# Modulation of the opening stage by unsplit fp32 products for five of eight channel tiles, a held engine order there, and transposes for the later modulation sums

## The chip, the cores and the metric

The kernel runs on one core of a Trainium2 chip. The metric is the time of one execution on that core in microseconds (us), as the median of the runs shown. The engines are named as the profile names them: PE (TensorE, the matrix engine) and PEld (its weight loads), DVE (VectorE), ACT (ScalarE), POOL (GpSimd) and SP (the queue that issues most transfers). SBUF is the core's working memory and PSUM the memory into which PE writes.

## What is computed

A two-layer backbone over 256 latent tokens and 256 context tokens of 1024 channels, all in fp32. Each layer has a modulated norm, a projection to a pooling branch and two attention branches, a gated merge, and a gated MLP. What the change touches is the modulation:

```python
mod   = (silu(c)     @ w_mod[l] + b_mod[l]).reshape(Bn, 6, 1, D_MODEL)
mod_c = (silu(c_ctx) @ w_mod[l] + b_mod[l]).reshape(6, 1, 1, D_MODEL)
h  = rms_norm(x, norm1_g[l])   * (1 + mod[:, 1]) + mod[:, 0]
hc = rms_norm(ctx, norm1_g[l]) * (1 + mod_c[1])  + mod_c[0]
z, zc = h @ w_in[l], hc @ w_in[l]
```

`w_mod` is 1024 by 6144 for each layer. There are two conditioning vectors, `c` and `c_ctx`, so every modulation value is a product of a matrix with two vectors.

## The kernel before

Tokens lie along the free axis (512 of them, latent then context, 256 each) and channels along the 128 partitions, in eight tiles of 128 channels. A large product is made in three passes of fp32r operands: weights are split into a high part `wH` (ACT, line 188) and a low part `wL` (line 190, on DVE or POOL), the normalised stream into `hH` (ACT, 470) and `hL` (DVE, 471), and `mm3` (205 to 207) adds high by high, high by low and low by high.

**Opening stage.** It turns `x` and `ctx` into channel tiles (`ptx`, 605; copies `xs`, 606), sums their squares on ACT (608), and forms the reciprocal root of the mean by three Newton steps (`rsqrt`, here on POOL, 294 to 297). `spread_b` (313, tile `rBp`) spreads the roots over the partitions. `rows_turn` (132) turns the biases into columns (`pt_a`). For each channel tile j, `first_mod(j)` loads 2 units of `w_mod` (512 rows by 256 columns: 128 columns of shift, 128 of scale), splits them, and multiplies: the conditioning vectors, 4 columns of high and low parts (`cHL`), are the weights, and 256 columns of `w_mod` stream, 16 products in all (`pm`, 344 and 345). ACT copies the 4 rows out (`mrow`, 348), PE turns them (`mt`, 357), and DVE adds bias and one and multiplies by the norm's gain (`mod`, 361 and 364). `start_apply(j)` makes `hu` (468), `hH` and `hL` of the tile, and the tile's part of the projection of the window branch (`pq` 512 wide, `pkv` 256 wide, 24 products for each tile) follows. The code runs `first_mod` up to two tiles ahead of the projection. `run_program` walks the list of steps, issues loads some units ahead (`MORE`) and splits `AHEAD` = 2 units ahead. The unit's number decides the engine of its low part: in this stage DVE, and POOL for numbers 5, 7 and 8:

```python
eng = pool_e if (self.idx % 4) in ONPOOL[self.lay] or self.idx in FPOOL else dve
```

A scheduler of the framework sets the order of each engine's instructions within the data's dependencies; `after` adds an order between two instructions of one engine.

**Later modulation.** The other 4 groups of layer 0 and all 6 of layer 1 are computed in the background of other products (`Background`): DVE multiplies and adds blocks of `w_mod` into `ma`, 128 partitions by 512 columns (431, 433), and `fin` sums over the partitions with 4 products by a column of ones (447, PSUM tile `mpt`), whose 4 columns DVE then finishes (453 to 460). `fin` runs 32 times. Its PSUM tile comes from a pool of two banks that transposes and spreads share (`psT`).

Of the kernel before, what the change touches and what calls it, by code (L numbers as in the profile page):

```python
# [32 lines left out]
ORD = 6  # L33
FPOOL = (5, 7, 8)
# [8 lines left out]
def kernel(  # L43
# [116 lines left out]
    lastop = {}  # L160
# [5 lines left out]

    class Unit:
        def __init__(self, load, kt, cols, first=False):
            self.load, self.kt, self.cols, self.first, self.loaded = load, kt, cols, first, False
            self.lay = now[0]  # L170
            self.uses, self.idx, self.H, self.L, self.side = 0, None, None, None, False

# [8 lines left out]
        def split(self):  # L181
# [36 lines left out]
    def run_program():  # L218
        units, loads, seen = [], [], set()
        cur = 0  # L220
        for need, _ in prog:
            for u in need:
                u.uses += 1
                if id(u) not in seen:
                    seen.add(id(u))
                    if u.side:
                        loads.append((cur + SIDE, u))
                    else:
                        cur = u.idx = len(units)
                        units.append(u)  # L230
                        loads.append((cur, u))
# [21 lines left out]
        for need, fn in prog:  # L253
# [5 lines left out]
            if started or need:  # L259
                split_to(cur + 1 + AHEAD)  # L260
# [11 lines left out]
    AHEAD = 2  # L272
# [15 lines left out]
    def rsqrt(v, n, name="rs", apart=False):  # L288
        r = small(n, f"{name}_r", 2)
        lastop["magic"] = dve.tensor_scalar(r.bitcast(I32), v.bitcast(I32), -0.5, float(0x5F3759DF), op0=ALU.mult, op1=ALU.add)  # L290
        t = small(n, f"{name}_t", 2)
        for _ in range(3):
            if apart:
                pool_e.tensor_tensor(out=t, in0=r, in1=r, op=ALU.mult)
                pool_e.tensor_tensor(out=t, in0=t, in1=v, op=ALU.mult)
                pool_e.tensor_scalar(t, t, -0.5, 1.5, op0=ALU.mult, op1=ALU.add)
                pool_e.tensor_tensor(out=r, in0=r, in1=t, op=ALU.mult)
            else:
                dve.tensor_tensor(out=t, in0=r, in1=r, op=ALU.mult)
# [1071 lines left out]
```

## Time and profile before

| | |
|---|---|
| median of 3 runs | 1394.54 us (1388.57 to 1395.63) |
| the profiled execution: its own time, its span | 1393.51 us, 1391.6 us |
| PE busy, DVE, ACT, POOL | 95%, 60%, 48%, 41% of the span |
| chain of work that ended last: PE, DVE, ACT | 78%, 11%, 4% |
| first product of the projection, first product after it | 35.10 us, 83.88 us |
| granted clock of PE over the span | 0.982 of full speed |

Busy shares are means over stages. The chain tells which engine's work the end waited for; the timeline of an engine tells when it started what and, in brackets, how long it had been idle and for whom; a table of stretches gives busy time and granted clock (0.50 is 1.2 GHz, 1.00 is 2.4 GHz). Records of PE overlap: the cost of one is the distance of the starts of neighbours, not its length. An fp32 product with fp32 weights shows as two records, one with fp32r operands and a transpose as one.

### The profile page before, as it was taken

How to read it: one execution, taken by the hardware profiler on the slowest of the kernel's cores; microseconds unless marked ns; L12 is line 12 of the kernel's file. 1: busy time of each engine (PE TensorE's matmuls, PEld its weight loads, DVE VectorE, ACT ScalarE, POOL GpSimd, SP SyncE). 2: the span in 40 equal slices, each digit the busy share in tenths (PEclk: the TensorE clock that was granted, in tenths of full speed). 3: DMA queues.
4: the chain of work that ended last, by engine and by line, in shares of the span. 5: the costliest groups of instructions: out<-in, count | busy, mean ns of one | idle time of the engine just before them, and what ended most of it. 6: DMA issues, size and time to landing. Idle time of an engine off the chain costs nothing.

```text
span 1391.6 us, 21515 instructions
## 1 busy us (share of the span) xinstructions
PE 1320.5 (95%) x8133; PEld 1160.0 (83%) x8133; DVE 841.8 (60%) x1766; ACT 664.6 (48%) x1238; POOL 573.8 (41%) x317
## 2 busy tenths in 40 slices
PE   4999899989999999999999999998999998999997
PEld 3877678868888898888888888987898898999997
DVE  6779965587765667766644333478818845544422
ACT  4558652257633344433433222457745854555442
POOL 4421223452234434444444343453246154566553
PEclk8999999999999999999999999999999998999999
DMA  9711124532135544555654554543154156466653
GB/s 282 234 39 61 61 81 139 174 92 93 61 119 150 176 132 121 167 157 163 182 165 151 160 174 152 163 142 120 54 144 140 58 180 184 135 183 183 197 160 99
DMA packets 174087, 195.75 MB, mean 141 GB/s; under 512 B 6878, under 2 KB 147830, under 8 KB 173728
## 3 DMA queue, kind: packets, MB, share of 16 engines
q1 hardware_dynamic: 173088, 193.23, 45.3%
q0 software_dynamic: 896, 1.14, 0.4%
q8 instruction: 64, 1.05, 0.3%
q14 instruction: 39, 0.32, 0.1%
HBM read 191.21 MB, written 3.15 MB: 140 GB/s over the span
## 4 chain that ended last, share of the span: by engine, by line
PE 78%; DVE 11%; ACT 4%; issue 3%; DMA 2%; POOL 2%; SPq 0%; ACTq 0%; POOLq 0%; DVEq 0%
PE gp L205 21%; PE gp L206 20%; PE gp L207 20%; PE mpt L447 2%; PE S L865 2%; PE ptp L906 2%; POOL wL L190 1%; PE pq L205 1%; DMA raw<-in_w_mod_dram 1%; PE pq L206 1%; DVE pr L895 1%; PE pq L207 1%; ACT wH L188 1%; PE O L206 1%; PE O L205 1%
## 5 line engine op out<-in xcount | busy, mean ns | idle before, releaser
L190 POOL TENSOR_TENSOR wL<-raw,wH 128x1024 fp32r<-128x1024 f32 (+2 forms) x233 | 541.9, 2330 | 773.1 <-ACT wH L188 685.5
L188 ACT ACTIVATE wH<-raw 128x1024 fp32r<-128x1024 f32 (+2 forms) x294 | 293.6, 1001 | 364.1 <-PE gp L206 177.7
L205 PE MATMUL gp<-hH,wH 128*128 128x512 f32 (+1 forms) x1168 | 394.8, 340 | 4.1 <-ACT hH L470 1.5
L206 PE MATMUL gp<-hL,wH 128*128 128x512 f32 (+1 forms) x1168 | 392.2, 336 | 1.6 <-DVE hL L471 1.6
L207 PE MATMUL gp<-hH,wL 128*128 128x256 f32 (+1 forms) x1168 | 391.5, 336 | 2.2 <-POOL wL L190 1.4
L205 PEld LDWEIGHTS gp<-hH,wH 128*128 128x128 f32 x1168 | 221.9, 191 | 25.8 <-ACT hH L470 2.3
L207 PEld LDWEIGHTS gp<-hH,wL 128*128 128x128 f32 x1168 | 222.4, 191 | 25.0 <-POOL wL L190 1.8
L206 PEld LDWEIGHTS gp<-hL,wH 128*128 128x128 f32 x1168 | 222.8, 191 | 22.8 <-DVE hL L471 2.7
L433 DVE SCALAR_TENSOR_TENSOR mb<-raw,cs,mb 128x512 f32<-128x512 f32 x182 | 131.0, 751 | 109.8 <-DMA raw<-in_w_mod_dram 108.9
L205 PE MATMUL gp<-g,wH 128*128 128x256 f32 (+1 forms) x396 | 128.1, 324 | 0.0
L206 PE MATMUL gp<-g,wH 128*128 128x256 f32 (+1 forms) x396 | 127.6, 322 | 0.0
L207 PE MATMUL gp<-g,wL 128*128 128x256 f32 (+1 forms) x396 | 127.4, 322 | 0.0
L190 DVE TENSOR_TENSOR wL<-raw,wH 128x1024 fp32r<-128x1024 f32 (+2 forms) x61 | 71.0, 1166 | 83.3 <-ACT wH L188 73.2
L207 PEld LDWEIGHTS gp<-g,wL 128*128 128x128 f32 x396 | 75.8, 191 | 6.1
L206 PEld LDWEIGHTS gp<-g,wH 128*128 128x128 f32 x396 | 75.9, 192 | 5.9
L205 PEld LDWEIGHTS gp<-g,wH 128*128 128x128 f32 x396 | 75.7, 191 | 5.9
L876 ACT ACTIVATE pr<-S,nm 128x512 f32<-128x512 f32 (+1 forms) x96 | 58.6, 611 | 18.2 <-DVE nm L871 9.9
L205 PE MATMUL gp<-y,wH 128*128 128x512 f32 (+1 forms) x192 | 67.3, 351 | 0.0
L207 PE MATMUL gp<-y,wL 128*128 128x512 f32 (+1 forms) x192 | 65.5, 342 | 1.0 <-POOL wL L190 1.0
L206 PE MATMUL gp<-y,wH 128*128 128x512 f32 (+1 forms) x192 | 65.9, 343 | 0.0
L871 DVE TENSOR_REDUCE nm<-S 128x1 f32<-128x512 f32 (+1 forms) x96 | 56.7, 594 | 10.4 <-PE S L865 7.4
L202 DVE TENSOR_TENSOR pL<-ptp,pH 128x512 fp32r<-128x512 f32 (+1 forms) x96 | 57.0, 595 | 7.1 <-ACT pH L201 6.6
(213 smaller groups left out, 2292.2 us busy)
## 6 DMA issues: line engine op xcount, KB each, us to landing
raw<-in_w_mod_dram SPq DMA_DIRECT2D x80, 512.0 KB, 3.8
raw<-in_w_gate_dram SPq DMA_DIRECT2D x48, 512.0 KB, 3.5
raw<-in_w_ff_gate_dram SPq DMA_DIRECT2D x44, 512.0 KB, 4.0
raw<-in_w_ff_val_dram SPq DMA_DIRECT2D x44, 512.0 KB, 3.9
raw<-in_w_ff_down_dram SPq DMA_DIRECT2D x44, 512.0 KB, 3.6
raw<-in_w_in_dram SPq DMA_DIRECT2D x32, 384.0 KB, 3.4
raw<-in_w_branch_dram SPq DMA_DIRECT2D x24, 512.0 KB, 3.4
raw<-in_w_mod_dram SPq DMA_DIRECT2D x32, 256.0 KB, 6.1
```

What stands on the lines that cost most here:

```text
L188: h = act.activation(out=self.H, in_=self.raw, func=AF.Copy)
L190: lo = eng.tensor_tensor(out=self.L, in0=self.raw, in1=self.H.bitcast(F32), op=ALU.subtract)
L202: dve.tensor_tensor(out=Lo, in0=src, in1=H.bitcast(F32), op=ALU.subtract)
L205: recent.append(pe.matmul(o, lhsT=aH, rhs=bH, start=first, stop=False))
L206: pe.matmul(o, lhsT=aH, rhs=bL, start=False, stop=False)
L207: pe.matmul(o, lhsT=aL, rhs=bH, start=False, stop=last)
L433: dve.scalar_tensor_tensor(out=S["a"][s], in0=raw, scalar=cs[:, s, k:k + 1], in1=S["a"][s], op0=ALU.mult, op1=ALU.add)
L447: pe.matmul(red[:, m:m + 1], lhsT=S["a"][s][:, m * P:(m + 1) * P], rhs=ones, start=(m == 0), stop=(m == 3))
L865: pe.matmul(S, lhsT=self.hd.qT[t][:, h], rhs=self.hd.kT[:, kv * 2 + v, koff:koff + nkey], start=(v == 0), stop=(v == 1 and not msk))
L871: dve.tensor_reduce(out=nm, in_=S, axis=AX.X, op=ALU.max, negate=True)
L876: act.activation(out=pr[:, :nkey], in_=S, func=AF.Exp, scale=0.125 if self.window else 1.0, bias=nm, accum_out=ls)
L906: pe.transpose(pt[:, k], pr[:, k * P:(k + 1) * P], ident)
```

## The change

For channel tiles 0, 1, 2, 4 and 6 (`PLAIN`) the weights of the modulation are no longer split. Blocks of 128 by 128 of raw `w_mod` are the weights of 16 fp32 products whose moving operand is the two conditioning vectors (`pmc`, 2 columns); the sums come out in channel order, so copy, turn and their additions fall away and two instructions on DVE finish them (`fin0`). Tiles 3, 5 and 7 keep the split. The order is held on PE (`pin`) and for the splits (`turned`, `hold`): the modulation of tile j + 1 stands inside the projection of tile j, after two of its four token blocks (after one for a split tile, whose turn follows one block later). Loads go by tile: `w_mod` of tile j, then `w_in` of tile j. The Newton steps go to DVE, the biases are turned before them, and the spread roots of tile 0 are read from PSUM. POOL splits nothing in this stage. The store of the stream to memory moves from tile 2 to tile 5 (`SPILL`). Later, `fin` turns its 4 blocks by transposes into a whole bank and DVE sums them (`tensor_reduce`). Since unsplit units are no longer numbered, the numbers of all later units fall by 10, which turns the pattern by which layer 1 gives low parts to POOL or DVE.

```diff
-ORD = 6
-FPOOL = (5, 7, 8)
+
+PLAIN = (0, 1, 2, 4, 6)
...
+    def pin(mm, at):
+        if at and "pe" in lastop:
+            after(mm, lastop["pe"])
+        lastop["pe"] = mm
...
-            eng = pool_e if (self.idx % 4) in ONPOOL[self.lay] or self.idx in FPOOL else dve
+            eng = pool_e if (self.idx % 4) in ONPOOL[self.lay] else dve
             lo = eng.tensor_tensor(out=self.L, in0=self.raw, in1=self.H.bitcast(F32), op=ALU.subtract)
-            if self.idx < ORD:
-                after(h, lastop["sq"])
-                if eng is dve:
-                    after(lo, lastop["magic"])
+            if self.tile is not None:
+                after(h, turned.get(max(turned) if self.first else self.tile - 1, lastop["sq"]))
+                after(lo, lastop["hold"])
...
                     if u.side:
-                        loads.append((cur + SIDE, u))
+                        loads.append((cur + SIDE if u.key is None else u.key, u))
                     else:
-                        cur = u.idx = len(units)
+                        u.idx = len(units)
+                        cur = u.idx if u.key is None else cur
                         units.append(u)
-                        loads.append((cur, u))
+                        loads.append((u.idx if u.key is None else u.key, u))
...
-            if started or need:
-                split_to(cur + 1 + AHEAD)
+            if started or any(not u.side for u in need):
+                split_to(cur + 1 + ahead[0])
...
-            if apart:
-                pool_e.tensor_tensor(out=t, in0=r, in1=r, op=ALU.mult)
...
+            dve.tensor_tensor(out=t, in0=r, in1=r, op=ALU.mult)
+            dve.scalar_tensor_tensor(out=t, in0=t, scalar=-0.5, in1=v, op0=ALU.mult, op1=ALU.mult)
+            lastop["hold"] = dve.scalar_tensor_tensor(out=r, in0=t, scalar=1.5, in1=r, op0=ALU.add, op1=ALU.mult)
...
+            w = Unit(load, 4, 256, True)
+            w.side, w.key, w.tile = plain, j - 0.5, j
+            return w
+
+
+        def step0(u, w):
+            def fn():
+                if u == 0:
+                    S["pm"] = psT((P, 2, 2), name="pmc")
+                for k in range(4):
+                    kk = u * 4 + k
+                    for i in range(2):
+                        mm = pe.matmul(S["pm"][:, i], lhsT=w.raw[:, k, i * P:(i + 1) * P], rhs=csv[:, kk],
+                                       start=(kk == 0 and i == 0), stop=(kk == KT - 1 and i == 1))
+                        pin(mm, k == 0 and i == 0)
+                lastop["mods"] = mm
+            return fn
...
+        def fin0():
+            dve.tensor_scalar(modv[0][0][:, j], S["pm"][:, 0], colsA[0][:, j:j + 1], None, op0=ALU.add)
+            dve.tensor_scalar(modv[0][1][:, j], S["pm"][:, 1], late["b1"][:, j:j + 1],
+                              colsA[0][:, 48 + j:49 + j], op0=ALU.add, op1=ALU.mult)
...
-                red = psT((P, 4), name="mpt")
+                pt = psT((P, 4, P), name="mpt")
                 for m in range(4):
-                    pe.matmul(red[:, m:m + 1], lhsT=S["a"][s][:, m * P:(m + 1) * P], rhs=ones,
-                              start=(m == 0), stop=(m == 3))
+                    pe.transpose(pt[:, m], S["a"][s][:, m * P:(m + 1) * P], ident)
+                red = small(4, "mred", 2)
+                dve.tensor_reduce(out=red, in_=pt, axis=AX.X, op=ALU.add)
...
-        r = spread_a(ssum, 4, True)
+        colsA[0] = rows_turn(*arow0)
+        late["b1"] = cst.tile([P, KT], F32, name="b1")
+        dve.tensor_scalar(late["b1"], colsA[0][:, KT:2 * KT], 1.0, None, op0=ALU.add)
+        late["r"] = spread_a(ssum, 4)
+
+    def start_spread():
+        pb = spread_b(late["r"], 4)
         for s in range(2):
-            pb = spread_b(r[:, 2 * s:2 * s + 2], 2)
             rB = sp0.tile([P, 256], F32, name=f"rB{s}")
-            act.activation(out=rB, in_=pb, func=AF.Copy)
+            act.activation(out=rB, in_=pb[:, s * 256:(s + 1) * 256], func=AF.Copy)
             rBs.append(rB)
-        colsA[0] = rows_turn(*arow0)
+        late["pb"] = pb
...
-    SPILL = 2
+    SPILL = 5
...
-                apply_h(j, slice(s * 256, (s + 1) * 256), s, modv[0][1], modv[0][0], rBs[s])
+                apply_h(j, slice(s * 256, (s + 1) * 256), s, modv[0][1], modv[0][0],
+                        rBs[s] if j else late["pb"][:, s * 256:(s + 1) * 256])
...
+    mods, fin = first_mod(0)
+    extend(mods[:1])
+    add(start_spread)
+    extend(mods[1:])
+    add(fin)
     add(start_apply(0))
-    fins[1] = first_mod(1)
     for j in range(KT):
-        if j + 2 < KT:
-            fins[j + 2] = first_mod(j + 2)
+        steps = proj_w.steps(j)
+        at = 2 if j + 1 in PLAIN else 1
+        extend(steps[:at])
+        if j == KT - 1:
+            add(lambda: ahead.__setitem__(0, 2))
         if j + 1 < KT:
-            add(fins[j + 1])
+            mods, fin = first.pop(j + 1, None) or first_mod(j + 1)
+            extend(mods)
+            if j + 1 not in PLAIN:
+                extend(steps[at:at + 1])
+                at += 1
+            elif j + 2 < KT and j + 2 not in PLAIN:
+                first[j + 2] = first_mod(j + 2)
+                for need, _ in first[j + 2][0]:
+                    add(lambda: None, need)
+            add(fin)
             add(start_apply(j + 1))
-        extend(proj_w.steps(j))
+        extend(steps[at:])
```

PE at the beginning, from the last `x` transposes on. `pm` are the split products, `pmc` the unsplit ones, the numbers behind `raw`, `wH` and `wL` those of buffers. Before:

```order
L605 MATMUL ptx<-ident,xn_158 128x128 x8
L313 MATMUL rBp<-ident,rs_r 128x128 x4
L132 MATMUL pt_a_245<-ident,rows_a_121 128x92
L344 MATMUL pm<-wH_267,cHL 4x256
L345 MATMUL pm<-wL_268,cHL 4x256
...
L345 MATMUL pm<-wL_345,cHL 4x256
L205 MATMUL pq<-wH,hH_99 128x512
L357 MATMUL mt<-ident,mrow 128x4 x2
```

Now:

```order
L638 MATMUL ptx<-ident,xn_158 128x128 x8
L132 MATMUL pt_a_218<-ident,rows_a_121 128x92
L351 MATMUL pmc<-cs,raw_238 128x2 x8
L317 MATMUL rBp<-ident,rs_r 128x128 x4
L351 MATMUL pmc<-cs,raw_241 128x2 x8
L211 MATMUL pq<-wH,hH_99 128x512
...
L215 MATMUL pkv<-wH,hL_107 128x256
L351 MATMUL pmc<-cs,raw_246 128x2 x8
L351 MATMUL pmc<-cs,raw_249 128x2 x8
L211 MATMUL pq<-wH,hH_99 128x512
```

Three tiles' modulation stood ahead of the first projection product; now one does, and the next tile's lies between the halves of the projection.

DVE in the same stretch, up to the first `hu`. Before:

```order
L307 TENSOR_SCALAR nv<-xss 128x4
L290 TENSOR_SCALAR rs_r<-nv 128x4
L190 TENSOR_TENSOR wL_268<-raw_249,wH_267 128x1024
...
L190 TENSOR_TENSOR wL<-raw,wH 128x768
L359 COPY mt<-mt 128x8
L361 SCALAR_TENSOR_TENSOR mod_0_139<-mt,cols_a_247 128x2
L361 SCALAR_TENSOR_TENSOR mod_1_140<-mt,cols_a_247 128x2
L364 TENSOR_SCALAR mod_1_140<-mod_1_140,cols_a_247 128x2
L468 SCALAR_TENSOR_TENSOR hu<-xs,mod_1_140,rB_238 128x256
```

Now:

```order
L134 COPY cols_a_220<-pt_a_218 128x92
L311 TENSOR_SCALAR nv<-xss 128x4
L645 TENSOR_SCALAR b_222<-cols_a_220 128x8
L300 TENSOR_SCALAR rs_r<-nv 128x4
L719 TENSOR_SCALAR bgh_862<-cols_a_220 128x24
L303 TENSOR_TENSOR rs_t<-rs_r 128x4
...
L305 SCALAR_TENSOR_TENSOR rs_r<-rs_t,rs_r 128x4
L378 TENSOR_SCALAR mod_0_139<-pmc,cols_a_220 128x2
L379 TENSOR_SCALAR mod_1_140<-pmc,b_222,cols_a_220 128x2
L499 SCALAR_TENSOR_TENSOR hu<-xs,mod_1_140,rBp 128x256 x2
```

The low parts have left the stretch ahead of `hu`, and the Newton steps have come in.

PE at a later sum, in the products of the branches of layer 0. Before:

```order
L206 MATMUL gp<-y_3532,wH 128x512
L207 MATMUL gp<-y_3531,wL 128x512
L447 MATMUL mpt<-ones,ma 128x1 x8
L205 MATMUL gp<-y_3531,wH 128x512
L206 MATMUL gp<-y_3532,wH 128x512
```

Now:

```order
L214 MATMUL gp<-y_3458,wH 128x512
L215 MATMUL gp<-y_3457,wL 128x512
L477 MATMUL mpt<-ident,ma 128x128 x8
L211 MATMUL gp<-y_3457,wH 128x512
L214 MATMUL gp<-y_3458,wH 128x512
```

Two sums still follow each other between the same products; eight transposes stand where eight products by ones stood.

## Rows read from the trace of the kernel before

**Rows 1.** The profile's page: span, busy time by engine, and the chain that ended last, by engine.

```profile
span 1391.6 us, 21515 instructions
PE 1320.5 (95%) x8133; PEld 1160.0 (83%) x8133; DVE 841.8 (60%) x1766; ACT 664.6 (48%) x1238; POOL 573.8 (41%) x317
...
PE 78%; DVE 11%; ACT 4%; issue 3%; DMA 2%; POOL 2%; SPq 0%; ACTq 0%; POOLq 0%; DVEq 0%
```

**Rows 2.** Stretches of the opening stage: start:end, length, busy us of PE, PEld, DVE, ACT and POOL (records), granted clock, DMA share, GB/s.

```profile
19.60:30.40 10.80, 9.61 (x59) 6.37 (x59) 6.88 (x8) 5.97 (x9) 3.45 (x2) 0.76 1.11 306
35.10:41.60 6.50, 6.50 (x20) 5.27 (x21) 6.16 (x13) 5.03 (x9) 4.22 (x8) 0.50 1.03 289
41.60:83.60 42.00, 42.00 (x267) 34.43 (x266) 30.93 (x66) 21.10 (x34) 16.46 (x24) 1.00 0.46 151
```

**Rows 3.** Timeline of PE up to the first product of the projection: start, length, what, and in brackets the idle time before it and who ended it.

```profile
19.63 2.07 PE L313 MATMUL rBp<-ident,rs_r 128*128 128x128 f32 x8 [7.53 <-POOL rs_r L297]
21.50 0.36 PE L132 MATMUL pt_a<-ident,rows_a 92*128 92x92 f32 x1
...
22.35 0.41 PE L345 MATMUL pm<-wL,cHL 128*4 128x256 f32 x1
22.56 0.41 PE L344 MATMUL pm<-wH,cHL 128*4 128x256 f32 x1
...
35.10 0.80 PE L205 MATMUL pq<-wH,hH 128*128 128x512 f32 x1 [4.72 <-ACT hH L470]
```

**Rows 4.** Timeline of DVE: the last copies and the beginning of the root, the first tile's modulation and `hu`, and the second tile's modulation.

```profile
11.26 1.89 DVE L606 COPY xs<-ptx 128x512 f32<-128x512 f32 x3 [0.16 <-PE ptx L605]
...
27.16 4.52 DVE L361 SCALAR_TENSOR_TENSOR mod<-mt,cols_a 128x2 f32<-128x2 f32 x2
31.71 2.27 DVE L364 TENSOR_SCALAR mod<-mod,cols_a 128x2 f32<-128x2 f32 x1
34.02 0.88 DVE L468 SCALAR_TENSOR_TENSOR hu<-xs,mod,rB 128x256 f32<-128x256 f32 x2
...
36.44 0.35 DVE L361 SCALAR_TENSOR_TENSOR mod<-mt,cols_a 128x2 f32<-128x2 f32 x2
```

**Rows 5.** Timeline of POOL: the last Newton step, and the three low parts that it makes in this stage.

```profile
19.38 0.20 POOL L297 TENSOR_TENSOR rs_r<-rs_r,rs_t 128x4 f32<-128x4 f32 x1
26.95 7.01 POOL L190 TENSOR_TENSOR wL<-raw,wH 128x1024 fp32r<-128x1024 f32 x3 [7.37 <-ACT wH L188]
```

**Rows 6.** Timeline of ACT: the high parts of the first two units of `w_mod`, which start when these have landed.

```profile
13.33 1.06 ACT L188 ACTIVATE wH<-raw 128x1024 fp32r<-128x1024 f32 x1 [1.61 <-DMA raw<-in_w_mod_dram]
15.13 1.06 ACT L188 ACTIVATE wH<-raw 128x1024 fp32r<-128x1024 f32 x1 [0.75 <-DMA raw<-in_w_mod_dram]
```

**Rows 7.** Timeline of PE at full clock: first product of one tile's projection, first of the next modulation, its turn, first product of the next projection; and the first product after the stage.

```profile
44.92 0.50 PE L205 MATMUL pq<-wH,hH 128*128 128x512 f32 x1
...
49.20 0.28 PE L344 MATMUL pm<-wH,cHL 128*4 128x256 f32 x1
...
51.12 0.28 PE L357 MATMUL mt<-ident,mrow 4*128 4x4 f32 x2
51.33 0.50 PE L205 MATMUL pq<-wH,hH 128*128 128x512 f32 x1
...
83.88 0.48 PE L205 MATMUL gp<-hH,wH 128*128 128x512 f32 x1
```

**Rows 8.** All instructions on the tile `mpt` (nanoseconds, shortest/median/longest, first and last start in us), and the timeline at its first pair of sums and at its last.

```profile
L447 PE MATMUL mpt<-ones,ma x256: 164/250/353, 226.4 to 1319.4; 128*128 128x1 f32 x128
...
226.37 1.84 PE L447 MATMUL mpt<-ones,ma 128*128 128x1 f32 x16
...
228.07 0.48 PE L205 MATMUL gp<-hH,wH 128*128 128x512 f32 x1
...
1318.14 1.66 PE L447 MATMUL mpt<-ones,ma 128*128 128x1 f32 x8 [1.77 <-ACT ma L439]
```

**Rows 9.** Transposes of fp32 blocks between products: all on the tile `ptk`, and one group of four on the timeline of PE with the product that follows it and the next but one.

```profile
L811 PE MATMUL ptk<-ident,kn x16: 270/272/327, 86.8 to 93.9; 128*128 128x128 f32 x16
...
89.96 0.60 PE L811 MATMUL ptk<-ident,kn 128*128 128x128 f32 x4
90.31 0.48 PE L205 MATMUL gp<-hH,wH 128*128 128x512 f32 x1
90.63 0.39 PE L206 MATMUL gp<-hL,wH 128*128 128x512 f32 x1
```

**Rows 10.** Stretches with the granted clock at half speed, columns as in rows 2: the first of the opening stage, and those around the last sum.

```profile
14.60:24.60 10.00, 4.65 (x21) 3.34 (x22) 4.97 (x6) 4.67 (x6) 4.37 (x8) 0.50 1.12 297
...
1318.50:1321.70 3.20, 3.20 (x16) 3.20 (x16) 0.34 (x2) 0.00 (x0) 1.53 (x1) 0.50 0.58 193
1321.90:1325.10 3.20, 3.20 (x17) 3.20 (x16) 0.00 (x0) 1.06 (x1) 1.74 (x1) 0.50 0.30 104
1325.40:1328.60 3.20, 3.20 (x29) 3.20 (x28) 0.69 (x1) 0.63 (x1) 0.34 (x1) 1.00 0.51 159
```

**Rows 11.** DVE: a reduction of 512 columns of PSUM (all, with busy us and mean ns), and two steps of a Newton iteration on its timeline.

```profile
L871 DVE TENSOR_REDUCE nm<-S 128x1 f32<-128x512 f32 x64 | 43.4, 682 | 6.9 <-PE S L865 4.2 <-PE S L869 2.3
...
1175.79 0.16 DVE L300 SCALAR_TENSOR_TENSOR rs_t<-rs_t,nv 128x2 f32<-128x2 f32 x1
1175.98 0.16 DVE L301 SCALAR_TENSOR_TENSOR rs_r<-rs_t,rs_r 128x2 f32<-128x2 f32 x1
```

More of the change, by code (lines that the diff above doesn't have):

```diff
@@ L159 @@
     now = [2]
-    lastop = {}
+    lastop, turned = {}, {}
     def after(ins, prev):
@@ L171, in __init__ @@
             self.uses, self.idx, self.H, self.L, self.side = 0, None, None, None, False
+            self.key, self.tile = None, None
         def dma(self):
@@ L205, in mm3 @@
         recent.append(pe.matmul(o, lhsT=aH, rhs=bH, start=first, stop=False))
+        if "mods" in lastop:
+            after(recent[-1], lastop.pop("mods"))
         pe.matmul(o, lhsT=aH, rhs=bL, start=False, stop=False)
-        pe.matmul(o, lhsT=aL, rhs=bH, start=False, stop=last)
+        lastop["pe"] = pe.matmul(o, lhsT=aL, rhs=bH, start=False, stop=last)
     prog = []
@@ L312, in spread_b @@
         for t in range(n):
-            pe.matmul(pb[:, t * P:(t + 1) * P], lhsT=r[:, t:t + 1].to_broadcast([P, P]), rhs=ident,
-                      start=True, stop=True)
+            lastop["pe"] = pe.matmul(pb[:, t * P:(t + 1) * P], lhsT=r[:, t:t + 1].to_broadcast([P, P]),
+                                     rhs=ident, start=True, stop=True)
         return pb
@@ L343, in fn @@
                     cw = cHL[:, kk].rearrange("p s h -> p (s h)")
-                    pe.matmul(pm, lhsT=cw, rhs=w.H[:, k, :], start=(kk == 0), stop=False)
-                    pe.matmul(pm, lhsT=cw, rhs=w.L[:, k, :], start=False, stop=(kk == 7))
+                    pin(pe.matmul(pm, lhsT=cw, rhs=w.H[:, k, :], start=(kk == 0), stop=False), k == 0)
+                    mm = pe.matmul(pm, lhsT=cw, rhs=w.L[:, k, :], start=False, stop=(kk == 7))
+                    pin(mm, False)
+                lastop["mods"] = mm
                 if u == 1:
@@ L351, in first_mod @@
             us.append(mk(u))
-            add(step(u, us[u]), [us[u]])
+        steps = [((us[u],), (step0 if plain else step)(u, us[u])) for u in range(2)]
+        def fin0():
+            dve.tensor_scalar(modv[0][0][:, j], S["pm"][:, 0], colsA[0][:, j:j + 1], None, op0=ALU.add)
+            dve.tensor_scalar(modv[0][1][:, j], S["pm"][:, 1], late["b1"][:, j:j + 1],
+                              colsA[0][:, 48 + j:49 + j], op0=ALU.add, op1=ALU.mult)
         def fin():
@@ L356, in fin @@
             for i in range(2):
-                pe.transpose(pt[:, i], S["row"][:, i * P:(i + 1) * P], ident[:4, :4])
+                mm = pe.transpose(pt[:, i], S["row"][:, i * P:(i + 1) * P], ident[:4, :4])
+                pin(mm, i == 0)
+            lastop["mods"] = mm
             mt = small(8, "mt", 2).rearrange("p (i s h) -> p i s h", i=2, s=2)
@@ L365, in fin @@
                               op0=ALU.add, op1=ALU.mult)
-        return fin
+        return steps, fin0 if plain else fin
     class Background:
@@ L467, in apply_h @@
         u = tmp((P, sl.stop - sl.start), name="hu")
-        dve.scalar_tensor_tensor(out=u, in0=X["k"][k][:, sl], scalar=G[:, k, s:s + 1], in1=rB,
+        lastop["hold"] = dve.scalar_tensor_tensor(out=u, in0=X["k"][k][:, sl], scalar=G[:, k, s:s + 1], in1=rB,
                                  op0=ALU.mult, op1=ALU.mult)
-        act.activation(out=hH[k][:, sl], in_=u, func=AF.Identity, bias=S[:, k, s:s + 1])
+        turned[k] = act.activation(out=hH[k][:, sl], in_=u, func=AF.Identity, bias=S[:, k, s:s + 1])
         lastop["apply"] = dve.scalar_tensor_tensor(out=hL[k][:, sl], in0=u, scalar=S[:, k, s:s + 1],
@@ L576, in steps @@
                 out=raw[:, 0], in_=w_in[self.l, g * P:(g + 1) * P, self.c0:self.c0 + 768]), 1, 768)
+            if self.c0 == 512 and self.l == 0:
+                w.key, w.tile = g, g
             out = []
```

24 lines of the change are left out of this document (8 added, 16 removed).

## The prediction

> **What bounds the kernel now.** I read the page first [rows 1]: PE is busy for 95% of the span and the chain of work that ended last lies on it for 78%, so where PE runs without a pause, taking records out of its queue shortens the end one for one, and work on DVE, ACT or POOL is free until PE waits for it. Then I took the opening stage by stretches and by the engines' timelines, since the change rewrites it. PE stands idle from 12.10 to 19.63 for the root that POOL computes [rows 3, 5], makes three tiles' modulation, and is idle again for 4.72 us until `hH` of tile 0 is there at 35.10 [rows 3]. What held `hH` up is on DVE: two additions on 128x2 took 4.52 us and a third 2.27, while POOL made three low parts from 26.95 to 33.96; the same two took 0.35 us for the next tile [rows 4, 5]. From 35.10 PE has no pause up to the first product behind the stage at 83.88 [rows 2, 7]. For 6.50 us of that the granted clock is 0.50 [rows 2]. Last, I looked at the later sums on `mpt` [rows 8].
>
> **The later sums.** 256 records of `mpt` [rows 8] are 32 sums of 4 fp32 products at two records each. A pair of sums (16 records) starts at 226.37 and the next product at 228.07: 1.70 us, 0.85 for one sum, 0.106 for a record. The change puts 4 transposes in place of 4 products. Four transposes start at 89.96 and the next product at 90.31; the one behind that starts 0.32 later, where 0.23 is the rule, so the group costs 0.35 + 0.09 = 0.44 us [rows 9]. That is 0.41 less for a sum and 32 x 0.41 = 13.1 us in all. Both of the first pair's neighbours follow without a pause, so this lies on the path. The reduction added on DVE costs 0.68 [rows 11], 32 x 0.68 = 21.8 us on an engine that is busy for 60% [rows 1]; I count it at nothing, because the sums are needed a whole group of products later; if the cover is gone, as where the sum before the last residual waits for ACT [rows 8], it takes back up to 0.68 a time. Bounds: 14.4 if the 0.08 us that the product behind a pair of sums loses is saved too, 6.5 if half of it is lost on DVE.
>
> The transposes of rows 9 last 272 ns each but start 0.11 us apart, and the sum above goes by the starts. The Trainium skill (TensorE: Matmul & The Clock Gate, section on the PE-mode transpose) gives about 275 ns for a 128x128 transpose in a kernel, which agrees with the length in rows 9 and not with the distance; by that price 128 transposes would cost 35 us and the change would lose 8 here.
>
> **The head of the opening stage.** New path to the first product of the projection. The first unit of `w_mod` has landed by 13.33, the second by 15.13 [rows 6]. Eight unsplit products are 16 records; I price them like `mpt`, the only fp32 products with as few columns: 16 x 0.106 = 1.70 us, 13.3 to 15.0. The root: copies end at 13.15 [rows 4], four small instructions take about 0.8, nine Newton steps at 0.195 from start to start [rows 11] 1.76, done at 15.75 instead of 19.6 [rows 5]. The spread, 8 records, 0.85, to 16.6; the second 8 products to 18.3. Two additions on DVE, 0.2 + 0.35, as nothing runs on POOL; from `hu` to the first product 1.08 as before (34.02 to 35.10) [rows 3, 4]: 20.0. This is 15.1 us earlier. The price of the split, the row copy and the turn is gone.
>
> **The rest of the stage.** A projection takes 4.28 us (44.92 to 49.20), a split modulation 1.92 + 0.21 = 2.13 (to 51.33) [rows 7]. Before, 8 projections and 5 modulations stood behind 35.10: 34.2 + 10.7 = 44.9, and with 6.50 us at half clock, 3.3 more, 48.2 of the 48.8 measured. Now 8 projections, 4 unsplit modulations at 32 x 0.106 = 3.40 and 3 split ones stand there: 34.2 + 13.6 + 6.4 = 54.2. So an unsplit tile costs PE 1.3 us more than a split one. Behind it, PE has half a projection (2.1) while DVE and ACT need 0.55 + 1.08 + the weights' low part; that covers it. Behind a turn there are 1.6 us of products against 2.1 of chain: 0.5 for each of three tiles, 1.6 in all with the first. 20.0 + 54.2 + 1.6 = 75.8, which is 8.1 before 83.9.
>
> **The clock.** This takes back most of it. The clock fell to 0.50 once PE had paused, and came back only at 24.6, five us after work began at 19.63, and at 41.6, 6.5 us after 35.10 [rows 2, 3, 10]. Around the last sum it fell after a pause of 1.77 and stayed at 0.50 to 1325.1 though PE was busy throughout, the beginning of it with products of one column [rows 8, 10]. At 0.50 everything takes twice as long (0.21 instead of 0.12 between `pm` records) [rows 3, 7]. The new head has pauses of 1.2, 0.8 and 1.7 us and between them little but products of two columns. I take the clock as low from there: the spread and the second half of the first products cost 0.85 + 1.70 more, and 5.0 to 6.5 us of projection at half clock lose 2.5 to 3.3, together 5.4. Then each of four stretches of 3.40 us holds only products of two columns; before, the longest such stretch is 1.70 [rows 8], at full clock, so no row shows what 3.40 do. A fall costs 2.5 to 3.4; the bounds are no fall and four, 0 to 13.6. I take two at 2.5, since rows 10 stand nearer to a fall than the pairs of rows 8 do: 75.8 + 5.4 + 5.0 = 86.2, 2.3 later than now.
>
> **Edits at nothing.** The weights' transfers go tile by tile; DMA share is 0.46 behind 41.6 [rows 2], and each lands a tile before its use. Raw buffers of tile 4 wait on SP for the products of tile 1, with `w_in` queued behind; two tiles of PE work cover that, and without it PE waits some 4 us. The store of the stream goes 15 us later on SP, read 200 us later. The three low parts that leave POOL, and the turned pattern of layer 1, move work of equal count between idle engines: plus or minus 2.
>
> **Sum.** -13.1 + 2.3 = -10.8. The profiled execution took 1393.51 for a span of 1391.6 [rows 1], 1.0 under the median of 1394.54; I add the change to the median: 1383.7, rounded 1384.
>
> **Rivals.** (1) The clock holds in the whole stage. For it: PE is never idle for long, and pairs of sums do not lower the clock [rows 8]. Against it: rows 10. The stage ends at 75.8: -8.1 - 13.1, 1373. [...] (2) Slower than before: the transposes don't overlap. If each costs its length, 0.272, a sum costs 1.09 instead of 0.85 and 32 lose 7.6; with the opening's 2.3 that is 1404. It decides from 0.21 for a transpose; rows 9 show 0.11. (3) The reduction comes on the path and half of the saving goes: 1394.5 - 6.5 + 2.3 = 1390. Against it: the share of DVE. (4) The clock stays at half in the whole opening stage: 22.5 + 2 x 54.2 + 1.6 = 132.5, 48.6 later, 1430. Against it: eight stretches of whole projections. That the change doesn't do what it says is excluded by the order of the instructions.
>
> **How the numbers follow.** Forecast 0.52, within it 1377 (no fall) to 1391 (three or four); rival 1 0.22; rival 2 0.04; rival 3 0.12; rival 4 0.03; the rest, 0.07, between 1385 and 1395. The range 1371 to 1391 holds the forecast but for a few hundredths, rivals 1 and 3, and leaves out rivals 2 and 4, the forecast's last falls and part of the rest, under 0.2. Half a per cent is 7 us, about what a measurement of this kernel can tell from no change: faster means under 1387.5. The forecast gives 0.47 of that, rival 1 0.22, the rest 0.04: 0.73. Within: 0.05 + 0.12 + 0.03 = 0.20. Slower: rivals 2 and 4, 0.07.
>
> **What would show it.** Sums: a group of 8 transposes on `mpt` with the next product 0.8 to 0.9 after its start; 1.3 or more would be rival 2, and pauses of PE behind it rival 3. Head: first `pq` at 20 with the clock at 1.00 or at 22.5 with 0.50. Products: 16 `pmc` in 3.4 us at full clock; if a record costs more than 0.106 my price is wrong. Clock: 0.50 in one to three stretches behind 30 us, each after a `pmc` stretch; none would be rival 1. End of the stage: first `gp` between 81 and 91. I would be wrong altogether if PE waited there for transfers or for DVE.

## The result and the profile after

The changed kernel takes 1401.34 us (median of 12 runs, 1394.68 to 1407.0) and the kernel before 1392.93 (12 runs, 1388.57 to 1395.63). The ratio is 1.006, 95% interval 1.0045 to 1.0075: slower by 8.4 us, where I had forecast 1384 and a range up to 1391. The profiled execution took 1404.54 with a span of 1402.8, 11.2 more than the span in [rows 1]. That is 2.8 more than the medians differ by, so the sizes read from the two traces below are those of this pair of executions.

The page of the profile after:

```profile
span 1402.8 us, 21359 instructions
PE 1328.5 (95%) x8075; PEld 1168.3 (83%) x8075; DVE 867.6 (62%) x1791; ACT 652.4 (47%) x1223; POOL 554.4 (40%) x302
...
PE 71%; DVE 16%; ACT 4%; DMA 4%; issue 3%; POOL 1%; SPq 0%; ACTq 0%; DVEq 0%; POOLq 0%
```

PE's share of the chain fell from 78% to 71% and DVE's rose from 11% to 16%: DVE, which I had counted as free, now sets more of the time. To see where, I lay the two traces side by side at the places that both have, the later sums on `mpt`. Timeline of PE before (start, length, what):

```profile
632.42 1.84 PE L447 MATMUL mpt<-ones,ma 128*128 128x1 f32 x16
...
863.04 0.95 PE L447 MATMUL mpt<-ones,ma 128*128 128x1 f32 x8
...
1017.92 0.95 PE L447 MATMUL mpt<-ones,ma 128*128 128x1 f32 x8
```

And after, with the product that follows the first group:

```profile
231.13 1.03 PE L477 MATMUL mpt<-ident,ma 128*128 128x128 f32 x8
231.92 0.47 PE L211 MATMUL gp<-hH,wH 128*128 128x512 f32 x1
...
632.21 1.03 PE L477 MATMUL mpt<-ident,ma 128*128 128x128 f32 x8
...
866.74 0.60 PE L477 MATMUL mpt<-ident,ma 128*128 128x128 f32 x4
...
1030.94 0.60 PE L477 MATMUL mpt<-ident,ma 128*128 128x128 f32 x4
...
1332.38 0.66 PE L477 MATMUL mpt<-ident,ma 128*128 128x128 f32 x4 [1.24 <-ACT ma L469]
```

| place | before | after | shift | gained (-) or lost on the way |
|---|---|---|---|---|
| first pair of sums [rows 8] | 226.37 | 231.13 | +4.8 | +4.8, opening stage |
| a pair in the gated merge | 632.42 | 632.21 | -0.2 | -5.0 |
| last sum in the MLP of layer 0 | 863.04 | 866.74 | +3.7 | +3.9 |
| a sum in layer 1 | 1017.92 | 1030.94 | +13.0 | +9.3 |
| last sum [rows 8] | 1318.14 | 1332.38 | +14.2 | +1.2 |
| end of the span | 1391.6 | 1402.8 | +11.2 | -3.0 |

So the sums do save PE time (0.79 for a pair that took 1.70), and three places lose it: the opening, the MLP of layer 0, and the beginning of layer 1. The clock has a part in all three. Read in stretches of 1 us over the whole span, PE runs at half speed for 78 us after and for 49 before; 31 of the 78 and 17 of the 49 lie in the opening stage. The 3.0 that come back at the end go with the half speed around the last sum [rows 10], which is gone: after, the clock stays at 1.00 from the last sum to 1395.

**Opening.** Timeline of PE:

```profile
20.00 0.79 PE L211 MATMUL pq<-wH,hH 128*128 128x512 f32 x1 [1.65 <-ACT hH L501]
...
23.91 4.07 PE L351 MATMUL pmc<-cs,raw 128*128 128x2 f32 x32
...
34.70 4.57 PE L351 MATMUL pmc<-cs,raw 128*128 128x2 f32 x32
...
52.83 3.63 PE L351 MATMUL pmc<-cs,raw 128*128 128x2 f32 x32
56.31 0.48 PE L211 MATMUL pq<-wH,hH 128*128 128x512 f32 x1
...
68.98 4.70 PE L351 MATMUL pmc<-cs,raw 128*128 128x2 f32 x32
73.54 0.77 PE L211 MATMUL pq<-wH,hH 128*128 128x512 f32 x1
...
88.54 0.47 PE L211 MATMUL gp<-hH,wH 128*128 128x512 f32 x1
```

And the stretches (columns as in [rows 2]), cut where the granted clock changes:

```profile
20.00:23.50 3.50, 3.50 (x10) 3.01 (x11) 1.46 (x3) 1.20 (x2) 2.40 (x5) 0.50 1.17 313
23.50:26.90 3.40, 3.40 (x32) 3.34 (x30) 0.00 (x0) 0.00 (x0) 1.81 (x4) 1.00 1.17 303
27.00:33.70 6.70, 6.70 (x22) 5.79 (x23) 4.09 (x8) 3.53 (x5) 3.83 (x6) 0.50 1.12 296
33.80:37.10 3.30, 3.30 (x30) 3.21 (x28) 0.00 (x0) 0.00 (x0) 2.84 (x12) 1.00 0.22 79
37.20:43.90 6.70, 6.70 (x26) 6.03 (x26) 4.00 (x8) 1.65 (x3) 0.00 (x0) 0.50 0.85 227
...
57.70:61.00 3.30, 3.30 (x13) 2.91 (x12) 1.77 (x4) 1.40 (x3) 0.00 (x0) 0.50 0.79 228
...
71.40:78.10 6.70, 6.70 (x25) 6.09 (x26) 2.95 (x7) 2.57 (x4) 0.00 (x0) 0.50 0.16 50
```

The first projection product stands at 20.00 and PE is busy from there for all but 0.3 us, yet the stage ends at 88.54, 4.7 later than before [rows 7]. The clock falls with each of the four long `pmc` stretches: inside three of them (at 26.9, 37.1 and 71.3, 2.3 to 3.0 us after their start) and, for the one at 52.83, 1.3 us behind its end. The 26.9 us of half speed in these rows lose 13.5; the remaining 55.1 of the 68.54 are my 54.2 of work at full speed within a microsecond.

### The profile page after: what moved, and what is told of

Its sections match the earlier page's. It is cut to its first block, busy times and chain, and to the rows that moved or that the text cites. A ratio compares the mean times of both kernels' runs of the same rounds, so it can differ in the third digit from the quotient of the medians.

```text
span 1402.8 us, 21359 instructions
## 1 busy us (share of the span) xinstructions
PE 1328.5 (95%) x8075; PEld 1168.3 (83%) x8075; DVE 867.6 (62%) x1791; ACT 652.4 (47%) x1223; POOL 554.4 (40%) x302
## 4 chain that ended last, share of the span: by engine, by line
PE 71%; DVE 16%; ACT 4%; DMA 4%; issue 3%; POOL 1%; SPq 0%; ACTq 0%; DVEq 0%; POOLq 0%
PE gp L211 18%; PE gp L215 18%; PE gp L214 18%; DMA raw<-in_w_mod_dram 3%; DVE ma L463 2%; PE ptp L960 2%; PE S L919 2%; DVE pr L949 1%; PE pmc L351 1%; PE pq L211 1%; PE O L214 1%; PE pq L214 1%; PE pq L215 1%; PE O L211 1%; PE O L215 1%
## 5 line engine op out<-in xcount | busy, mean ns | idle before, releaser
L197 POOL TENSOR_TENSOR wL<-raw,wH 128x1024 fp32r<-128x1024 f32 (+3 forms) x230 | 532.7, 2322 | 797.7 <-ACT wH L195 744.0
L195 ACT ACTIVATE wH<-raw 128x1024 fp32r<-128x1024 f32 (+2 forms) x284 | 282.4, 999 | 316.2 <-PE gp L214 157.8
L197 DVE TENSOR_TENSOR wL<-raw,wH 128x1024 fp32r<-128x1024 f32 (+3 forms) x54 | 60.7, 1127 | 97.4 <-ACT wH L195 77.3
L930 ACT ACTIVATE pr<-S,nm 128x512 f32<-128x512 f32 (+1 forms) x96 | 58.6, 611 | 21.9 <-DVE nm L925 11.2
```

Source lines behind the costliest of these rows:

```text
L195: h = act.activation(out=self.H, in_=self.raw, func=AF.Copy)
L930: act.activation(out=pr[:, :nkey], in_=S, func=AF.Exp, scale=0.125 if self.window else 1.0, bias=nm, accum_out=ls)
```

## Experiments

Each kernel was timed against the kernel before on its chip; the time of before is given where it is needed, and a ratio is one to that time. "Theory A" and its rivals are those of the expectation that stands ahead of each result.

### The later sums on DVE

All instructions on `mred` after (nanoseconds, shortest/median/longest):

```profile
L479 DVE TENSOR_REDUCE mred<-mpt x32: 678/684/693, 231.8 to 1333.1; 128x4 f32<-128x512 f32 x32
L488 DVE TENSOR_TENSOR mred<-mred,cols_a x12: 150/155/2119, 233.0 to 1333.8; 128x4 f32<-128x4 f32 x12
...
L491 DVE TENSOR_TENSOR mod<-mred,cols_a x10: 151/158/2360, 415.1 to 814.2; 128x4 f32<-128x4 f32 x10
```

The reduction costs 0.68, as forecast. The small additions behind it now take up to 2.36 instead of 0.16. Timelines of DVE and of POOL at one of them:

```profile
642.62 2.36 DVE L491 TENSOR_TENSOR mod<-mred,cols_a 128x4 f32<-128x4 f32 x1
```

```profile
642.57 2.39 POOL L197 TENSOR_TENSOR wL<-raw,wH 128x1024 fp32r<-128x1024 f32 x1 [5.18 <-ACT wH L195]
```

It starts 0.05 behind a low part on POOL and lasts until that ends. Of 54 such additions 11 start inside a low part of POOL, and 10 of these take 0.4 to 2.4, 17.8 us in all (nine have two inputs in SBUF, one, of 2.11 at 586.65, is a `tensor_scalar` with one); before, 19 do, reading `mpt` in PSUM, and none takes over 0.17. PE's waits from 640 to 885 after (none is listed before):

```profile
PE gp L211 <- DVE fa L1293: 6.3, 5, 1.7
```

One kernel takes the sums alone:

```diff
-                red = psT((P, 4), name="mpt")
...
+                pt = psT((P, 4, P), name="mpt")
...
+                red = small(4, "mred", 2)
+                dve.tensor_reduce(out=red, in_=pt, axis=AX.X, op=ALU.add)
```

> The kernel before with the later sums by transposes and nothing else. Theory A (the sums save about 12 us on PE, but DVE, which reduces and finishes them, comes late in the gated MLP of layer 0 and PE waits there for about 7 us): 1388, with waits of PE for the gate's sums (fa) between 640 and 890 us. Rival B (the sums cost nothing on DVE, as I forecast, and those waits come from the opening or from the counting of units): 1381 and no such waits. Rival C (the sums lose): over 1393.

Measured 1387.61 (before 1391.88; ratio 0.9966, 0.995 to 0.9982). The waits are there without the opening and without the new counting; same view, up to 879:

```profile
PE gp L205 <- DVE fa L1240: 6.1, 5, 1.7
```

Theory A holds. In both kernels the clock also falls once among these waits (half speed from 658 to 662 after, from 651 to 654 here); before, and in the next two kernels, it doesn't. Two kernels then keep the reduced sums in PSUM, in the changed kernel and in the kernel before:

```diff
-                red = small(4, "mred", 2)
+                red = pt[:, 0, :4]
```

> The changed kernel with the reduced sums kept in PSUM (in the bank of the transposes) in place of SBUF, so that the additions behind them read PSUM. Theory A (10 of 44 such additions took about 2 us because both operands were in SBUF while POOL worked, 18 us of DVE, and this makes PE wait in the MLP of layer 0): all of them at 0.15 to 0.17 us, PE's waits between 640 and 890 fall from 7 us to 2 or less, time 1396. Rival B (the reductions of 0.68 alone make DVE late): additions short, waits as before, 1401.

> The kernel before with the later sums by transposes and the reduced sums kept in PSUM. Theory A (the slow additions on SBUF are what brings the waits in the MLP of layer 0, worth 4 us as in the changed kernel): 1384, the waits there at 2 us or less. Rival B (the reductions do it): 1387.6 as with the sums in SBUF.

Measured 1397.31 (before 1391.88; ratio 1.0039, 1.0022 to 1.0056) and 1380.89 (before 1392.76; ratio 0.9919, 0.9898 to 0.994): 4.0 less than the changed kernel and 6.7 less than the sums in SBUF. Set against the kernel before of their own runs these are 3.0, where the intervals of the two ratios overlap, and 7.6, where they don't. The longest addition is 0.171 in both. (The count is 54, not the 44 of the expectation.) The waits up to 879, of the first and of the second:

```profile
PE gp L211 <- DVE fa L1293: 3.7, 4, 1.2
```

```profile
PE gp L205 <- DVE fa L1240: 2.0, 2, 1.2
```

Theory A had 2 us or less for both. So the blocked additions are the larger part of the wait in the kernel before with new sums (6.1 to 2.0) and less than half in the changed kernel (6.3 to 3.7); what is left may come from the reductions, whose removal was not tried.

### The pattern of the low parts

Timeline of PE after, and of DVE there:

```profile
932.83 0.79 PE L214 MATMUL pq<-wL,hH 128*128 128x512 f32 x1 [3.93 <-DVE wL L197]
```

```profile
927.02 4.50 DVE L502 SCALAR_TENSOR_TENSOR hL<-hu,mod,hH 128x256 fp32r<-128x256 f32 x4 [0.41 <-ACT hH L501]
931.44 0.47 DVE L499 SCALAR_TENSOR_TENSOR hu<-xs,mod,rBp 128x256 f32<-128x256 f32 x1
931.83 0.95 DVE L197 TENSOR_TENSOR wL<-raw,wH 128x768 fp32r<-128x768 f32 x1
```

The turned pattern gives DVE the second block of the projection's weights, which PE needs at once and which on DVE stands behind the tiles of `hL`. Those four take 4.50, where a single one takes 0.47 at 932.70, and POOL makes low parts beside them:

```profile
926.66 1.84 POOL L197 TENSOR_TENSOR wL<-raw,wH 128x768 fp32r<-128x768 f32 x1 [2.70 <-ACT wH L195]
929.20 2.04 POOL L197 TENSOR_TENSOR wL<-raw,wH 128x768 fp32r<-128x768 f32 x1 [0.69 <-ACT wH L195]
```

So DVE looks blocked by POOL here as it is in the additions above, but no run tested this; in the kernel before the same four take 3.31. The old pattern was put into the changed kernel, and the turned one into the kernel before:

```diff
-            eng = pool_e if (self.idx % 4) in ONPOOL[self.lay] ...
+            eng = pool_e if ((self.idx + 2) % 4) in ONPOOL[self.lay] ...
```

> The changed kernel with the old pattern of POOL and DVE for the low parts (two added to the unit's number). Theory A (the turned pattern puts low parts on DVE where it is late, and that costs most of the 11 us lost between 900 and 1200 us): about 1391, and PE's wait of 3.9 us for a low part made by DVE near 932 is gone. Rival B (the loss there is the phase of the clock and late loads, the pattern is worth nothing, as I forecast): 1401.

> The kernel before with the turned pattern of POOL and DVE (two added to the unit's number) and nothing else. Theory A (the pattern alone costs what restoring it gave back, 10.8 us): 1403, with PE's wait for a low part made by DVE near 920 us. Rival B (it costs only together with the later sums or the new opening): 1392 to 1396.

Measured 1390.5 (before 1391.88; ratio 0.9987, 0.9972 to 1.0001), and 1408.18 (before 1392.76; ratio 1.0105, 1.0082 to 1.0127). Restoring the pattern gives back 10.8 (9.8 against the kernel before of its own runs), turning it alone costs 15.4, and the wait moves with it. It is gone in the first and stands in the second:

```profile
933.58 0.80 PE L206 MATMUL pq<-wL,hH 128*128 128x512 f32 x1 [3.95 <-DVE wL L190]
```

The wait is only a part of what the pattern costs. From 866 to the sum in layer 1, PE's idle time is 16.3 us after and 11.2 before, and half speed is 17.1 us after (from 921.2, 931.4 and 962.1), 17.1 with the pattern turned alone, 10.2 with the old pattern put back, and 3.4 before. Over the whole span the kernel with the pattern turned alone runs at half speed for 70 us, before for 49. Which fall of the clock goes back to which wait is not shown.

### The opening stage and the clock

The opening alone (old sums, old pattern):

> The kernel before with the new opening stage alone: sums by ones as before, old pattern of POOL and DVE. Theory A (the parts add up: the stage ends 4.7 later in the profile, and nothing behind it changes): 1396 to 1398. Rival B (the opening is worth nothing and the rest of the loss is interaction): 1393 or less.

Measured 1401.48 (before 1391.85; ratio 1.0055, 1.0036 to 1.0074): dearer than theory A. The stage ends at 88.80, with three stretches at half speed, 26.3 us in all (from 20.4, 40.1 and 60.6), and the other 4.2 of the 9.1 by which the span grew to 1400.7 are lost behind it, where half speed lasts 39 us against 32 before (worth up to 3.6). The same opening does not give the same falls in every kernel: here the clock stays down from 16.2 to 36.7, and the last long `pmc` stretch (at 72.33) brings no fall, as in the changed kernel with the sums in PSUM (at 74.02).

Two kernels test what lowers the clock: one takes the long stretches away, one cuts them.

```diff
-PLAIN = (0, 1, 2, 4, 6)
+PLAIN = (0,)
```

> The changed kernel with unsplit products for tile 0 alone, tiles 1 to 7 split. Theory A (the stretches of 3.4 us of two-column products behind the first projection lower the clock, 27 us at half speed from 20 us on, and cost PE 1.3 us more each than split ones): the clock rises once and stays up, the stage ends at 20.0 + 2.6 + 8 x 4.28 + 7 x 2.13 + some 3 for turns = 75 in place of 88.5, time about 1388. Rival B (the stage is bound by transfers or by the splits on ACT and DVE once the products go faster): PE waits in it, end at 82 to 88, 1395 to 1401. Rival C (the clock falls all the same): half speed shown behind 25 us, end at 83 to 86.

Measured 1396.82 (ratio 1.004, 1.0025 to 1.0056). Stretches, and one projection product on the timeline of PE:

```profile
20.00:23.70 3.70, 3.70 (x14) 3.32 (x15) 3.66 (x5) 2.90 (x4) 2.68 (x6) 0.50 1.16 319
23.80:78.20 54.40, 46.56 (x287) 34.74 (x285) 38.24 (x74) 26.73 (x41) 16.43 (x23) 1.00 0.72 210
78.40:81.70 3.30, 2.81 (x9) 2.44 (x10) 1.51 (x7) 1.08 (x2) 0.34 (x5) 0.50 0.46 159
```

```profile
44.50 0.50 PE L211 MATMUL pq<-wH,hH 128*128 128x512 f32 x1 [0.96 <-ACT hH L501]
```

The clock stays up to 78.2, as theory A has it, and falls once, at the end of a wait of PE of 1.8 us. But PE is busy for only 46.6 of 54.4: each tile waits about 1 us for the turn, the copy and `hH`, which the other order of work had hidden, and the stage ends at 83.81. Theory A's time does not come, rival B's does (the waits are mostly for `hH`). In the second kernel the 16 products stand as 8 and 8 (of tiles 4 and 6 the first 8 in the projection before):

```diff
-        at = 2 if j + 1 in PLAIN else 1
-        extend(steps[:at])
+        extend(steps[:1])
...
+        else:
+            mods, fin = first_mod(j + 1)
+            extend(mods[:1])
+            extend(steps[1:3])
+            extend(mods[1:])
...
+            extend(steps[3:])
```

> The changed kernel with the same instructions, but each block of 16 unsplit products behind the first projection product cut into two of 8 with projection between them, so that PE never makes such products for over 1.7 us in a row. Theory A (it is the long stretches that lower the clock): no or one fall between 25 and 88 us where there were four, and the stage ends near 77 to 80 with some 2 us of waits at tiles 1 and 2; time about 1391. Rival B (the products lower the clock in whatever pieces, or their weight loads do): three or four falls, end at 86 to 90, 1400. Rival C (the clock holds, but PE waits for the weights or for the new modulation): gaps of PE of 5 us and more, end at 83 to 86.

Measured 1401.46 (ratio 1.0063, 1.0044 to 1.0082), no gain. Stretches, and two of the cut blocks on the timeline of PE:

```profile
22.00:40.50 18.50, 18.30 (x69) 16.66 (x69) 7.05 (x13) 4.82 (x8) 14.35 (x26) 0.50 0.75 209
40.60:47.30 6.70, 6.31 (x46) 5.67 (x46) 1.91 (x5) 0.98 (x3) 0.00 (x0) 1.00 0.59 165
47.40:50.70 3.30, 3.30 (x14) 2.40 (x14) 0.94 (x3) 0.56 (x1) 0.00 (x0) 0.50 0.93 267
50.80:88.00 37.20, 37.20 (x249) 32.23 (x248) 22.95 (x51) 16.38 (x27) 5.05 (x6) 1.00 0.50 165
```

```profile
24.72 3.41 PE L351 MATMUL pmc<-cs,raw 128*128 128x2 f32 x16
...
54.07 1.84 PE L351 MATMUL pmc<-cs,raw 128*128 128x2 f32 x16
```

Both theories get a part: behind 50.8 the clock holds through tiles 4 and 6, but beside the cut products of tiles 1 and 2 it stays down for 18.5 us and, once up, falls again at 47.3, 2 us behind the last of them. The stage ends at 88.25. The next kernel therefore splits tiles 1 and 2 as well (with the old pattern and the sums in PSUM):

> As the woven opening with the old pattern and the sums in PSUM, but tiles 1 and 2 are split too, so that unsplit products in pieces of 1.7 us stand only in tile 0 and, once the clock is up, in tiles 4 and 6. Theory A (pieces of 1.7 us with projection around them let a clock that is up stay up, but keep one that is down from coming back, which is what held half speed from 17 to 41 us in the woven kernel): half speed ends by 28 us and does not come back before 280; stage end near 79 with about 1 us of waits at each split tile, some 7 us earlier than with tiles 1 and 2 unsplit, time 1379. Rival B (the pieces lower the clock in any case): falls at tiles 4 and 6, end at 83 to 86, 1384 to 1387.

Measured 1380.12 (ratio 0.9908, 0.9892 to 0.9924). Half speed ends by 27.5, returns once, and the stage ends at 81.41: theory A but for that one fall.

```profile
48.10:51.30 3.20, 3.20 (x10) 2.61 (x9) 2.86 (x4) 2.10 (x3) 0.00 (x0) 0.50 1.04 308
```

It comes right behind the first cut block of tile 4 (46.00 to 47.70), so what theory A says of a clock that is up does not always hold. The last question was the wait of 1 us for each split tile. Tile 0 alone is unsplit, and the modulation of tile j + 2 is made in the projection of tile j:

> Tile 0 unsplit, tiles 1 to 7 split with the modulation of each made most of a projection ahead of its use (the 16 products stand behind the third token block of the tile before the last), the old pattern, and the sums in PSUM. Theory A (with the clock up and the turn off the path, PE is the bound of the stage): no wait of over 0.5 us behind the first projection product, half speed ends by 28 us, stage end at 20.0 + 1.8 + 8 x 4.28 + 7 x 2.13 = 71 to 74, time 1380.9 - 10 to 12 = 1369 to 1371. Rival B (ACT, DVE or the transfers can't split the weights at that pace): waits of PE for the high or low parts, 7.7 us for a tile as with tile 0 alone unsplit, end at 80 to 84, 1378 to 1381.

Measured 1383.29 (ratio 0.9933, 0.9914 to 0.9951), the stage ends at 86.59, later than both theories have it, and the waits are there still, for `hH` and not for the parts of the weights:

```profile
47.65 0.50 PE L211 MATMUL pq<-wH,hH 128*128 128x512 f32 x1 [0.95 <-ACT hH L501]
```

The split of the next weights was held, on ACT and DVE, behind the normalised values of the tile before, so that the products could not run ahead. `lead2` moves that hold back by a tile and lets splits run two units ahead:

```diff
-                after(h, turned.get(max(turned) if self.first else self.tile - 1, lastop["sq"]))
-                after(lo, lastop["hold"])
+                t = max(self.tile - (2 if self.first else 1), 0)
+                after(h, turned.get(t, lastop["sq"]))
+                after(lo, holds.get(t, lastop["hold"]))
...
-    ahead = [0]
+    ahead = [2]
```

> As the kernel with the modulation made a projection ahead, but the splits of a tile's modulation weights are no longer held behind the normalised values of the tile before, only of the one before that. Theory A (it was this order of ACT and DVE that kept the products from running ahead; with it gone PE is the bound): no wait of 0.9 us a tile behind the first projection product, stage end at 72 to 76, some 8 to 10 before the 83.8 of the kernel with before's opening and the sums in PSUM: 1371 to 1373. Rival B (ACT, DVE or transfers bound the stage at 7.7 us for a tile): end at 80 to 84, 1378 to 1381.

Measured 1370.66 (before 1391.85; ratio 0.9842, 0.9821 to 0.9862), faster than both kernels. Stretches, and the first product behind the stage:

```profile
21.30:26.70 5.40, 5.33 (x21) 4.18 (x22) 5.35 (x5) 4.60 (x6) 4.22 (x8) 0.50 1.14 312
26.80:74.00 47.20, 46.65 (x297) 37.68 (x296) 38.58 (x79) 26.07 (x43) 14.75 (x24) 1.00 0.73 223
```

```profile
74.31 0.48 PE L212 MATMUL gp<-hH,wH 128*128 128x512 f32 x1
```

PE is busy for 46.65 of 47.20 at full clock, so theory A holds: the early head (first projection product at 21.37) is worth 9.5 us at the end of the stage once nothing takes it back. Which of the two edits did it, the hold or the two units, was not separated.

### Do the parts add up?

Woven opening, old pattern and sums in PSUM together:

> The changed kernel with the woven opening, the old pattern of POOL and DVE, and the reduced sums in PSUM. Theory A (three separate causes that add up: 10 for the clock, 10.8 for the pattern, 4 for the additions): 1401.3 - 25 = 1376, faster than both kernels. Rival B (they overlap, since a fall of the clock or a wait that one removes comes back elsewhere): 1384 to 1390.

Measured 1386.32 (before 1392.76; ratio 0.9949, 0.9933 to 0.9966): rival B. The woven opening brought nothing by itself, so only 15 of theory A's 25 were there to add. The parts alone, against the kernel before of their runs, are -4.3 (sums), +9.6 (opening) and +15.4 (pattern), 20.7 together, where the change costs 8.4. Beside the opening the sums are worth 11.0 (1401.48 to 1390.5), not 4.3, and beside the rest the pattern costs 10.8, not 15.4. By the spans of the profiled executions, sums alone give 8.2 (1391.6 to 1383.4) and beside the opening 10.5 (1400.7 to 1390.2), so the gap between 4.3 and 11.0 is not certain. Why the parts do not add up stays open; the falls of the clock, which come at other places in every kernel, are a likely reason that was not tested.

## Why the prediction was wrong

- **The later sums on PE: right.** 1.70 became 0.79 for a pair; from the start of each of the 21 groups to PE's next record, 28.1 us became 16.2, a saving of 11.9 against 13.1. Transposes cost their distance, not their length, and rival 2 fell.
- **"I count it at nothing" (the reduction on DVE): wrong, and this is the first step that failed.** The 32 reductions took 0.68 as forecast, but I had read DVE's load as a mean over the span. In the MLP of layer 0 they and the additions come between DVE's sums for the gate, and PE waits 6.3 us there. The step also looked at the reduction only. The additions behind it moved from PSUM to SBUF, and ten of them, blocked by POOL, took 17.8 us. [Rows 4] had shown just this: 4.52 for two additions of SBUF values while POOL made low parts, 0.35 without. I used that row for the head of the opening and did not ask which other additions would now be like it. The Trainium skill (SBUF — State Buffer, section on SBUF's two separate sides) says that a DVE instruction with two SBUF inputs and a GpSimd instruction that reads SBUF exclude each other for the whole length of the one that started first; the 2.36 beside 2.39 above agrees. The `tensor_scalar` with one SBUF input, which took 2.11, is not in that sentence. Rival 3 had this as a mechanism with 6.5 left of the saving; measured alone, 4.3 was left.
- **"Work of equal count between idle engines: plus or minus 2" (the turned pattern): wrong, and the dearest step.** It cost 10.8 here and 15.4 alone. The count per engine is nearly the same (59 low parts on DVE with the pattern turned alone, 61 before, 233 on POOL in both), but which weights go to DVE is not, and an engine that is idle on the mean stands 4.5 us deep in `hL` where the second block of the projection comes. The wait of 3.9 there is the part that is shown; with it come other waits and more half speed, which I had not in the sum at all.
- **The head: right at its end, in part by luck.** First projection product at 20.00, with the clock at half; I had 20.0 with the clock held and counted 22.5 for this case. The clock fell only at 16.6, so it cost about 0.9 and not 2.5 (the second 8 products took 2.58 instead of 1.70, the spread went at full speed), and a root that was ready 1.0 earlier (the spread starts at 14.79, I had 15.75) made up for that.
- **The rest of the stage at full speed: right.** 54.2 forecast, 55.1 measured; 32 two-column records took 3.48 (52.83 to 56.31) against 3.40. The 1.6 of waits behind turns did not come.
- **"I take two at 2.5" (the clock): right in kind, too small.** Of the 10.4 for the start and two falls, 7.9 stood behind the first projection product. There were four falls (three of 6.8 us and one of 3.4, which is a cost of 3.4 and of 1.7), and with the start half speed behind 20.00 cost 13.5. The stage ended at 88.54 instead of 86.2. Behind the stage I had no change of the clock, and there half speed grew from 32 us to 47.
- **The sum.** The forecast was -10.8 and the result +8.4. Of the 19.2 between, the pattern is about 10.8, the waits in the MLP of layer 0 are 6.3 by the profile, and the opening 2.4 (4.7 against 2.3 at its end). This accounts for the size, but the parts measured alone do not add up, so it is one way to divide it and not the only one: alone, the opening cost 9.6, not 2.3.

## What to carry to other kernels

A renumbering is an edit: where a number picks the engine, list which work lands on which engine at the places where the next engine waits, not how much. Before a result moves from PSUM to SBUF, or a reduction to an engine with 40% to spare, look at that engine's queue in the stage where it will run, and at what POOL does there. An early start pays only as far as the stage behind it keeps its pace: here 15 us at the head were worth nothing with the clock down or the splits held back, and with both mended 14 at the head gave 9.5 at the end of the stage.

## What the runs showed of the hardware

- Long stretches of two-column fp32 products (32 records, PE never pausing) brought a fall of the clock from full speed to half in most cases: all four in the changed kernel, 2.3 to 3.0 us after the start of the stretch or 1.3 behind its end; in two other kernels with the same opening the last stretch brought none. With only tile 0 unsplit the clock fell once, in a wait. Whether it is the two columns, the fp32 weights or their loads was not tested.
- In pieces of 1.84 (8 products) with projection between them the clock stayed up in some places (50.8 to 88.0 in the woven kernel) and fell in others, 0.3 to 2.1 us behind a piece: at 47.3 there, at 48.0 with tiles 1 and 2 split, at 34.6 and 44.9 with the parts together. Three of these four have a short wait of PE (0.4 to 0.8) beside them. When the clock was down, it stayed down for 18.5 us beside the same pieces.
- At half speed such a record costs nearly twice as long as at full speed: 16 take 3.41 at 24.72 in the woven kernel and 1.84 at 54.07.
- A DVE addition of 128x4 in SBUF lasted 2.36 beside a POOL instruction of 2.39; the same addition reading PSUM took at most 0.171 beside POOL.
- Eight transposes of 128x128 took 0.79 from the first start to the next product, 0.10 each, though each record lasts 0.27.
